# Two tiles per instruction, and copies for every quadrant move, in a batched matmul with bias and residual

## The chip, the cores and the metric

The kernel runs on one core of one Trainium2 chip. Times are device microseconds of one execution. A core has five engines with instruction queues of their own: TensorE (PE, with its weight load PEld), VectorE (DVE), ScalarE (ACT), GpSimd (POOL) and SyncE (SP), which here only issues DMA transfers.

## The reference

```python
batch, m, k, n = 16, 512, 1024, 768        # all float32
out = np.matmul(x, weight) + bias + residual
```

x is 16 x 512 x 1024, so 8192 rows of 1024; weight is 1024 x 768; residual and out are 8192 rows of 768. x is 33.6 MB, residual and out 25.2 MB each, the weight 3.1 MB.

## The kernel before

**Tiles, batches, groups.** The 8192 rows are 64 tiles of 128 rows. Four tiles are a batch (B = 4), eight a group (G = 8). Partition p of a group holds eight consecutive rows of DRAM, and tile j of the group is row j of every partition. x, residual and output are transferred by groups: 4.19 MB for x, 3.15 MB for the others, all issued from SyncE's queue, which issues in program order and waits in front of an issue until its buffer is ready.

**From x to the stationary operand.** TensorE needs x with the contraction on the partitions. Each batch is cast to bf16 by ScalarE (`cast_x`, L110, one cast for each quarter of the contraction, 128x1024 elements), in an order that puts neighbouring contraction elements in pairs, so that two bf16 can be moved as one 32-bit word. VectorE then transposes blocks of 32x32 words, and the blocks are moved between quadrants of 32 partitions. There are sixteen moves (q, m), of 32 partitions x 512 words each. For quarters 0 and 1 VectorE transposes all 128 partitions at once into `tq` (`transpose_blocks`, L124), and ScalarE makes the eight moves as copies (`move_blocks`, L132). For quarters 2 and 3 VectorE transposes each block straight into its place (`transpose_and_move`, L140, eight instructions a batch). The result `xt` has two buffers, `xb` and `tq` one each.

**Matmul and evacuation.** For each tile `matmul` (L149) accumulates eight steps of the contraction in PSUM, each in two chunks, 512 and 256 columns wide. There are four PSUM buffers of a tile each. `evacuate` adds the residual on VectorE (L168) in place in the residual's buffer, and GpSimd then adds the bias (L174, `add_bias`). In group 0 the residual isn't loaded yet: VectorE adds the bias into `o_tile` (L165), and GpSimd adds the residual later (`add_residual`, L178). The bias of the last two tiles is added ahead of time.

**Buffers.** x has two group buffers; the last residual (`r_last`) uses one of them. Four homes of a group each hold the rest: `HOME = [0, 1, 3, 0, 1, 2, 3]` gives the home of residual groups 0 to 6; home 2 starts as `o_tile`, home 3 as the weight's staging buffer. So the load of residual group 3 waits until the last `add_residual` has read group 0 out of home 0, and the load of group 4 until group 1 has been stored.

**Order.** The order on each engine is the program's, written out by hand. In batch b: the matmuls of tile 4b, the whole transposes for batch b+1, the evacuation of the tile before, ScalarE's moves for b+1 and two casts for b+2; then the matmuls of the other three tiles, between which VectorE transposes quarters 2 and 3 into place and evacuates one tile each time. `add_residual` comes at the end of batches 2 and 3, four tiles each, in GpSimd's queue between the bias adds. Transfers follow a table:

```python
moves = {
    1: [(load_x, 3)],
    3: [(load_x, 4), (load_r, 3)],
    4: [(store, 1)],
    5: [(load_x, 5), (load_r, 4), (store, 0)],
    7: [(load_x, 6), (load_r, 5), (store, 2)],
    9: [(load_x, 7), (load_r, 6)],
    11: [(load_r, 7), (store, 3), (store, 4)],
    12: [(store, 5)],
    14: [(store, 6)],
}
```

The functions that the change touches, and what calls them:

Of the kernel before, what the change touches and what calls it, by code (L numbers as in the profile page):

```python
# [7 lines left out]
FP32 = mybir.dt.float32  # L8
BF16 = mybir.dt.bfloat16
U32 = mybir.dt.uint32  # L10
P = 128
Q = 32
G = 8
B = 4
X_BUFS = 2
HOME = [0, 1, 3, 0, 1, 2, 3]
PO_BUFS = 4


@with_exitstack  # L20
def kernel(
# [8 lines left out]
    nc = tc.nc  # L30
# [3 lines left out]
    M, K = x2d.shape  # L34
    N = weight.shape[1]
    R = K // P
    KQ = K // 4
    n_sub = M // P
    n_grp = n_sub // G
    n_bat = n_sub // B  # L40
    chunks = [(0, 512), (512, N - 512)]

    def group(ap, g):

        return ap[g * G * P:(g + 1) * G * P, :].rearrange("(p j) k -> p j k", p=P)

    const = ctx.enter_context(tc.tile_pool(name="const", bufs=1))
    xin_pool = ctx.enter_context(tc.tile_pool(name="xin", bufs=1))
    ring_pool = ctx.enter_context(tc.tile_pool(name="ring", bufs=1))
    xb_pool = ctx.enter_context(tc.tile_pool(name="xbp", bufs=1))  # L50
    xt_pool = ctx.enter_context(tc.tile_pool(name="xtp", bufs=1))
    po_pool = ctx.enter_context(
        tc.tile_pool(name="pop", bufs=1, space=bass.MemoryType.PSUM))

    def o(ins):
        return tc.keep_in_program_order(ins)

    count = {}

    def slot(pool, base, n, shape, dtype, name=None):  # L60
        i = count.get(base, 0)
        count[base] = i + 1
        return pool.tile(shape, dtype, name=name or base, tag=f"{base}{i % n}", bufs=1)

    def home(i, name):
        return ring_pool.tile([P, G, N], FP32, name=name, tag=f"ring{i}", bufs=1)


    bias_rows = const.tile([P, N], FP32, name="bias_rows")
    o(nc.gpsimd.memset(bias_rows, 0.0))  # L70
    warm = const.tile([1, 2], FP32, name="warm")
    o(nc.vector.memset(warm, 0.0))
# [2 lines left out]
    bias_bc = const.tile([P, N], FP32, name="bias_bc")  # L75


    x_tiles, r_tiles, o_tiles = {}, {}, {}

    def load_x(g, j0=0, j1=G):  # L80
        if g not in x_tiles:
            x_tiles[g] = slot(xin_pool, "x_tile", X_BUFS, [P, G, K], FP32)
        o(nc.sync.dma_start(out=x_tiles[g][:, j0:j1, :], in_=group(x2d, g)[:, j0:j1, :]))
# [10 lines left out]
    def store(g, j0=0, j1=G):  # L94
        src = o_tiles[g] if g == 0 else r_tiles[g]
        o(nc.sync.dma_start(out=group(out2d, g)[:, j0:j1, :], in_=src[:, j0:j1, :]))
# [3 lines left out]

    xb_tiles, tq_tiles, xt_tiles, po_tiles = {}, {}, {}, {}

    def cast_x(b, q):

        if b >= n_bat:
            return
        g, j = divmod(b * B, G)
        xb = slot(xb_pool, f"xb{q}_", 1, [P, B, R // 2, Q, 2], BF16)
        part = x_tiles[g][:, j:j + B, q * KQ:(q + 1) * KQ]
        o(nc.scalar.copy(out=xb, in_=part.rearrange("p t (a j r) -> p t j a r", j=R // 2, r=2)))  # L110
        xb_tiles[b, q] = xb.rearrange("p t j a r -> p (t j a r)").bitcast(U32).rearrange(
            "p (t j a) -> p t j a", t=B, j=R // 2)

    def xt_tile(b):
        if b not in xt_tiles:
            xt_tiles[b] = slot(xt_pool, "xt", 2, [P, B, R // 2, P], U32)
        return xt_tiles[b]

    def transpose_blocks(b, q):

        if b >= n_bat:
            return
        tq_tiles[b, q] = slot(xt_pool, f"tq{q}_", 1, [P, B, R // 2, Q], U32)
        o(nc.vector.transpose(out=tq_tiles[b, q], in_=xb_tiles.pop((b, q))))  # L124

    def move_blocks(b, q):

        if b >= n_bat:
            return
        xt, tq = xt_tile(b), tq_tiles.pop((b, q))  # L130
        for m in range(P // Q):
            o(nc.scalar.copy(out=xt[q * Q:(q + 1) * Q, :, :, m * Q:(m + 1) * Q],  # L132
                             in_=tq[m * Q:(m + 1) * Q]))

    def transpose_and_move(b, q):
        if b >= n_bat:
            return
        xt, xb = xt_tile(b), xb_tiles.pop((b, q))
        for m in range(P // Q):
            o(nc.vector.transpose(out=xt[q * Q:(q + 1) * Q, :, :, m * Q:(m + 1) * Q],  # L140
                                  in_=xb[m * Q:(m + 1) * Q]))

    def matmul(t):
        b, i = divmod(t, B)
        xt = xt_tiles[b].bitcast(BF16)[:, i].rearrange("p j (m r) -> p j r m", r=2)
        po_tiles[t] = slot(po_pool, "po", PO_BUFS, [P, N], FP32)
        for k in range(R):
            for (n0, nl) in chunks:
                o(nc.tensor.matmul(  # L149
                    po_tiles[t][:, n0:n0 + nl],  # L150
                    lhsT=xt[:, k // 2, k % 2, :],
                    rhs=w_sb[:, k, n0:n0 + nl],
                    start=(k == 0),
                    stop=(k == R - 1),
                ))

    def evacuate(t):


        if t < 0:  # L160
            return
        g, j = divmod(t, G)
        po = po_tiles.pop(t)
        if g == 0:
            o(nc.vector.tensor_add(out=o_tiles[0][:, j, :], in0=po, in1=bias_bc))  # L165
        else:
            rt = r_tiles[g][:, j, :]
            o(nc.vector.tensor_add(out=rt, in0=po, in1=rt))  # L168
            if t < n_sub - 2:
                add_bias(t)  # L170

    def add_bias(t):
        rt = r_tiles[t // G][:, t % G, :]
        o(nc.gpsimd.tensor_add(out=rt, in0=rt, in1=bias_bc))  # L174

    def add_residual(t):
        ot = o_tiles[0][:, t, :]
        o(nc.gpsimd.tensor_add(out=ot, in0=ot, in1=r_tiles[0][:, t, :]))  # L178


    for p in range(0, P, Q):
# [6 lines left out]
    load_r(1)  # L188
    o_tiles[0] = home(2, "o_tile")
    o(nc.vector.stream_shuffle(out=bias_bc, in_=bias_rows, mask=[0] * 32))  # L190
    for q in range(4):
        cast_x(0, q)
    for q in (0, 1):
        transpose_blocks(0, q)
    for q in (2, 3):
        transpose_and_move(0, q)
    for q in (0, 1):
        move_blocks(0, q)
    for k in range(R):
        if k % 2:  # L200
            o(nc.scalar.copy(out=w_sb[:, k, :], in_=w_stage[:, k, :]))  # L201
        else:
            o(nc.vector.tensor_copy(out=w_sb[:, k, :], in_=w_stage[:, k, :]))  # L203
    for q in range(4):
        cast_x(1, q)
    load_x(2)
    load_r(0)
    load_r(2)
# [13 lines left out]
    for b in range(n_bat):  # L222
        t = B * b
        matmul(t)
        for q in (0, 1):
            transpose_blocks(b + 1, q)
        evacuate(t - 1)
        for q in (0, 1):
            move_blocks(b + 1, q)
        for q in range(4):  # L230
            if q < 2:
                cast_x(b + 2, q)
        matmul(t + 1)
        transpose_and_move(b + 1, 2)
        evacuate(t)
        cast_x(b + 2, 2)
        matmul(t + 2)
        transpose_and_move(b + 1, 3)
        evacuate(t + 1)
        cast_x(b + 2, 3)  # L240
        matmul(t + 3)
        evacuate(t + 2)
        if b in (2, 3):
            for u in range(B * (b - 2), B * (b - 1)):
                add_residual(u)
        if b == n_bat - 3:
            for u in (n_sub - 2, n_sub - 1):
                add_bias(u)
        if b == n_bat - 1:
            store(n_grp - 1, 0, B)  # L250
        for move, *what in moves.get(b, []):
            move(*what)
    evacuate(n_sub - 1)
    store(n_grp - 1, B, B + 2)
    store(n_grp - 1, B + 2, G)
# [1 line left out]
_INS = ['x', 'weight', 'bias', 'residual']  # L257
# [26 lines left out]
```

## Time and profile before

| | |
|---|---|
| median of 3 runs | 211.26 us (210.24 to 211.74) |
| the profiled execution's own time | 210.11 us |
| its span, first to last instruction | 208.3 us |
| mean granted TensorE clock | 0.974 |
| busy: TensorE, VectorE, ScalarE, GpSimd | 171.5, 171.0, 151.4, 115.3 us |
| main transfer queue | 87.03 MB, 97.9% of 16 engines' span |
| HBM | 61.88 MB read, 25.17 MB written |

How to read the rows. A row of digits cuts the span into 40 slices of 5.2 us; a digit is the busy share in tenths, 9 being 90% or more. A group's line names the source line, engine, operation and operands, then "busy us, mean ns of one | idle time of the engine just before them, and what ended it". A line of a timeline has start, duration, engine, source line, operation, operands and how many instructions were merged; an idle time before it stands in brackets with its releaser. The waits of the queue are in us: total, times, longest. `SPq` lines are the issues of transfers, not the transfers themselves.

### The profile page before, as it was taken

The page shows a single profiled execution, that of the slowest core. Times are in us where ns is not written, and L with a number is a line of the kernel's source. Part 1 is how long each engine was busy: PE and PEld are TensorE (multiplying, and loading weights), DVE is VectorE, ACT ScalarE, POOL GpSimd, SP SyncE. Part 2 cuts the span into 40 slices and gives each one's busy share as a digit, 9 for nine tenths or more (in the row PEclk, how much of TensorE's full clock was granted, in tenths as well). Part 3 has the DMA queues.
Part 4 walks back from the last instruction along what each step waited for, and adds up shares of the span by engine and source line. Part 5 has one row for each costly group of instructions (what it writes and reads, how often), then busy time and mean ns, then how long its engine had stood idle before and what let it go on. Part 6 is the DMA issues. An engine that isn't in the chain of part 4 may idle for free.

```text
span 208.3 us, 2737 instructions
## 1 busy us (share of the span) xinstructions
PE 171.5 (82%) x1004; PEld 101.2 (49%) x1024; DVE 171.0 (82%) x231; ACT 151.4 (73%) x198; POOL 115.3 (55%) x69
## 2 busy tenths in 40 slices
PE   0002999999999999999999599996999589999940
PEld 0001566666666656565656256663656246666620
DVE  0089799999999999999995999949997699997320
ACT  2499999999797599897979579783979569750000
POOL 1000000003899999999764493916766376699900
PEclk9999999999999999999999979999999969999996
DMA  6999999999999999999999999999999999999995
GB/s 245 452 409 437 466 415 403 475 400 431 423 458 409 415 469 373 411 434 437 437 406 444 440 437 417 417 445 442 425 423 415 448 426 437 415 448 415 430 405 211
DMA packets 4053, 87.22 MB, mean 419 GB/s; under 512 B 452, under 2 KB 452, under 8 KB 712
## 3 DMA queue, kind: packets, MB, share of 16 engines
q1 hardware_dynamic: 4032, 87.03, 97.9%
q8 instruction: 8, 0.13, 0.2%
q14 instruction: 5, 0.04, 0.0%
q10 hardware_dynamic: 8, 0.01, 0.0%
HBM read 61.88 MB, written 25.17 MB: 418 GB/s over the span
## 4 chain that ended last, share of the span: by engine, by line
DMA 44%; DVE 26%; PE 16%; POOL 5%; issue 3%; ACT 2%; SPq 0%; ACTq 0%; DVEq 0%
DMA out_dram<-r_tile 20%; PE po L149 16%; DVE xt L140 14%; DMA out_dram<-o_tile 12%; DMA r_tile<-in_residual_dram 8%; DMA bias_rows<-in_bias_dram 4%; DVE r_tile L168 4%; POOL o_tile L178 3%; DVE o_tile L165 3%; POOL r_tile L174 2%; DVE w_sb L203 1%; ACT L73 1%; ACT xb__132 L110 1%; ACT xb__136 L110 0%; DVE bias_bc L190 0%
## 5 line engine op out<-in xcount | busy, mean ns | idle before, releaser
L149 PE MATMUL po<-w_sb,xt 128*128 128x512 bf16 (+1 forms) x1004 | 171.5, 331 | 28.5 <-DVE w_sb L203 19.8
L149 PEld LDWEIGHTS <-xt 128*128 128x128 bf16 x1024 | 101.2, 99 | 98.5 <-ACT w_sb L201 19.2
L174 POOL TENSOR_TENSOR r_tile<-r_tile,bias_bc 128x768 f32<-128x768 f32 x48 | 86.0, 1814 | 82.6 <-DVE r_tile L168 82.6
L168 DVE TENSOR_TENSOR r_tile<-po,r_tile 128x768 f32<-128x768 f32 x48 | 44.4, 946 | 9.1 <-DMA r_tile<-in_residual_dram 8.4
L178 POOL TENSOR_TENSOR o_tile<-o_tile,r_tile 128x768 f32<-128x768 f32 x8 | 14.3, 1825 | 0.0
L174 POOL TENSOR_TENSOR r_last<-r_last,bias_bc 128x768 f32<-128x768 f32 x8 | 14.3, 1810 | 0.0
L168 DVE TENSOR_TENSOR r_last<-po,r_last 128x768 f32<-128x768 f32 x8 | 7.5, 955 | 6.2 <-PE po L149 6.1
L190 DVE LOAD_MASK_SELECT bias_bc<-bias_rows x1 | 0.0, 14 | 10.3 <-DMA bias_rows<-in_bias_dram 10.3
L165 DVE TENSOR_TENSOR o_tile<-po,bias_bc 128x768 f32<-128x768 f32 x8 | 7.4, 945 | 0.1
L110 ACT CAST xb__95<-x_tile 128x1024 bf16<-128x1024 f32 x1 | 1.1, 1107 | 6.0 <-DMA x_tile<-in_x_dram 6.0
L132 ACT COPY xt<-tq__1018 32x512 uint32<-32x512 uint32 x4 | 2.5, 618 | 1.4 <-DVE tq__1018 L124 1.3
L132 ACT COPY xt<-tq__1232 32x512 uint32<-32x512 uint32 x4 | 2.5, 617 | 1.4 <-DVE tq__1232 L124 1.3
L132 ACT COPY xt<-tq__1552 32x512 uint32<-32x512 uint32 x4 | 2.5, 617 | 1.4 <-DVE tq__1552 L124 1.3
L132 ACT COPY xt<-tq__1659 32x512 uint32<-32x512 uint32 x4 | 2.5, 617 | 1.4 <-DVE tq__1659 L124 1.3
L132 ACT COPY xt<-tq__1337 32x512 uint32<-32x512 uint32 x4 | 2.5, 617 | 1.4 <-DVE tq__1337 L124 1.3
L132 ACT COPY xt<-tq__1446 32x512 uint32<-32x512 uint32 x4 | 2.5, 617 | 1.4 <-DVE tq__1446 L124 1.3
L132 ACT COPY xt<-tq__474 32x512 uint32<-32x512 uint32 x4 | 2.5, 616 | 1.4 <-DVE tq__474 L124 1.3
L132 ACT COPY xt<-tq__1123 32x512 uint32<-32x512 uint32 x4 | 2.5, 616 | 1.4 <-DVE tq__1123 L124 1.3
L132 ACT COPY xt<-tq__587 32x512 uint32<-32x512 uint32 x4 | 2.5, 618 | 1.4 <-DVE tq__587 L124 1.3
L132 ACT COPY xt<-tq__908 32x512 uint32<-32x512 uint32 x4 | 2.5, 616 | 1.4 <-DVE tq__908 L124 1.3
L110 ACT CAST xb__1299<-x_tile 128x1024 bf16<-128x1024 f32 x1 | 1.1, 1137 | 3.0 <-DVE xt L140 3.0
L110 ACT CAST xb__1513<-x_tile 128x1024 bf16<-128x1024 f32 x1 | 1.1, 1131 | 2.9 <-DVE xt L140 2.9
(158 smaller groups left out, 244.0 us busy)
## 6 DMA issues: line engine op xcount, KB each, us to landing
x_tile<-in_x_dram SPq DMA_DIRECT2D x7, 4096.0 KB, 23.2
r_tile<-in_residual_dram SPq DMA_DIRECT2D x7, 3072.0 KB, 17.0
out_dram<-r_tile SPq DMA_DIRECT2D x6, 3072.0 KB, 20.7
x_tile<-in_x_dram SPq DMA_DIRECT2D x2, 2048.0 KB, 13.1
w_stage<-in_weight_dram SPq DMA_DIRECT2D x1, 3072.0 KB, 14.4
out_dram<-o_tile SPq DMA_DIRECT2D x1, 3072.0 KB
r_last<-in_residual_dram SPq DMA_DIRECT2D x1, 3072.0 KB, 15.7
out_dram<-r_last SPq DMA_DIRECT2D x1, 1536.0 KB, 8.9
```

Source lines behind the costliest of these rows:

```text
L73: o(nc.scalar.copy(out=warm, in_=warm))
L110: o(nc.scalar.copy(out=xb, in_=part.rearrange("p t (a j r) -> p t j a r", j=R // 2, r=2)))
L132: o(nc.scalar.copy(out=xt[q * Q:(q + 1) * Q, :, :, m * Q:(m + 1) * Q], in_=tq[m * Q:(m + 1) * Q]))
L140: o(nc.vector.transpose(out=xt[q * Q:(q + 1) * Q, :, :, m * Q:(m + 1) * Q], in_=xb[m * Q:(m + 1) * Q]))
L149: o(nc.tensor.matmul(po_tiles[t][:, n0:n0 + nl], lhsT=xt[:, k // 2, k % 2, :], rhs=w_sb[:, k, n0:n0 + nl], start=(k == 0), stop=(k == R - ...
L165: o(nc.vector.tensor_add(out=o_tiles[0][:, j, :], in0=po, in1=bias_bc))
L168: o(nc.vector.tensor_add(out=rt, in0=po, in1=rt))
L174: o(nc.gpsimd.tensor_add(out=rt, in0=rt, in1=bias_bc))
L178: o(nc.gpsimd.tensor_add(out=ot, in0=ot, in1=r_tiles[0][:, t, :]))
L203: o(nc.vector.tensor_copy(out=w_sb[:, k, :], in_=w_stage[:, k, :]))
```

## The change

ScalarE casts two tiles in one instruction, the whole contraction at once (two casts of 128x2048 elements for a batch in place of four of 128x1024). VectorE transposes all 128 partitions of both halves (two instructions of 128x1024 words), and there is no transpose into place any more: all sixteen moves are copies, of which VectorE makes the first nine and ScalarE the last seven. `tq` holds a whole batch. A PSUM buffer holds two tiles, and there are two of them; evacuations and GpSimd's adds take two tiles in one instruction, the last two tiles apart. In a batch VectorE evacuates the pair before, transposes, copies, and then evacuates the batch's first pair. All adds of residual group 0 are issued on GpSimd in batch 2, ahead of the bias adds of tiles 8 and on. The bias rows' staging takes home 0 in place of a buffer of its own. The table of transfers is the same.

```diff
-PO_BUFS = 4
+H = 2
...
-    KQ = K // 4
+    J = R // 2
...
-    bias_rows = const.tile([P, N], FP32, name="bias_rows")
+    bias_rows = home(0, "bias_rows")[:, 0, :]
...
-    def cast_x(b, q):
+    def cast_x(b, h):
         if b >= n_bat:
             return
...
+        g, i = divmod(b * B + h * H, G)
+        xb = slot(xb_pool, f"xb{h}_", 1, [P, H, J, P, 2], BF16)
+        o(nc.scalar.copy(out=xb, in_=x_tiles[g][:, i:i + H, :].rearrange(
+            "p t (c j r) -> p t j c r", j=J, r=2)))
+        xb_tiles[b, h] = xb.rearrange("p t j c r -> p (t j c r)").bitcast(U32)
+
+    def transpose_blocks(b, h):
...
+        if h == 0:
+            tq_tiles[b] = slot(xt_pool, "tq", 1, [P, B * J * P], U32)
+        n = H * J * P
+        o(nc.vector.transpose(out=tq_tiles[b][:, h * n:(h + 1) * n], in_=xb_tiles.pop((b, h))))
+
+    def move_blocks(b, engine, n):
...
+            xt_tiles[b] = slot(xt_pool, "xt", 2, [P, B * J, P], U32)
+        tq = tq_tiles[b].rearrange("p (tj q a) -> p tj q a", q=P // Q, a=Q)
+        for _ in range(n):
+            i = count.get(("move", b), 0)
+            count["move", b] = i + 1
+            q, m = divmod(i, P // Q)
+            out_ = xt_tiles[b][q * Q:(q + 1) * Q, :, m * Q:(m + 1) * Q]
+            in_ = tq[m * Q:(m + 1) * Q, :, q, :]
+            if engine is nc.scalar:
+                o(engine.copy(out=out_, in_=in_))
+            else:
+                o(engine.tensor_copy(out=out_, in_=in_))
...
-        po_tiles[t] = slot(po_pool, "po", PO_BUFS, [P, N], FP32)
+        if t % H == 0:
+            po_tiles[t // H] = slot(po_pool, "po", 2, [P, H, 1024], FP32)
+        po = po_tiles[t // H][:, t % H, :]
...
+    def bias_for(n):
+        return bias_bc[:, None, :].broadcast_to([P, n, N])
+
+    def evacuate(t, n=H):
...
+        po = po_tiles[t // H][:, t % H:t % H + n, :N]
         if g == 0:
+            o(nc.vector.tensor_add(out=o_tiles[0][:, i:i + n, :], in0=po, in1=bias_for(n)))
         else:
+            rt = r_tiles[g][:, i:i + n, :]
             o(nc.vector.tensor_add(out=rt, in0=po, in1=rt))
             if t < n_sub - 2:
+                add_bias(t, n)
...
+    def add_bias(t, n=H):
+        i = t % G
+        rt = r_tiles[t // G][:, i:i + n, :]
+        o(nc.gpsimd.tensor_add(out=rt, in0=rt, in1=bias_for(n)))
+
+    def add_residual(t, n=H):
+        ot = o_tiles[0][:, t:t + n, :]
+        o(nc.gpsimd.tensor_add(out=ot, in0=ot, in1=r_tiles[0][:, t:t + n, :]))
...
+    for h in (0, 1):
+        cast_x(0, h)
+        transpose_blocks(0, h)
+    move_blocks(0, nc.vector, 9)
+    move_blocks(0, nc.scalar, 7)
...
+    for h in (0, 1):
+        cast_x(1, h)
...
         matmul(t)
...
         matmul(t + 1)
+        evacuate(t - H)
+        if t == G:
+            for u in range(0, G, H):
+                add_residual(u)
+        transpose_blocks(b + 1, 0)
+        transpose_blocks(b + 1, 1)
+        move_blocks(b + 1, nc.vector, 9)
+        move_blocks(b + 1, nc.scalar, 7)
+        cast_x(b + 2, 0)
+        matmul(t + 2)
+        matmul(t + 3)
         evacuate(t)
+        cast_x(b + 2, 1)
         if b == n_bat - 3:
+            add_bias(n_sub - 2)
...
-    evacuate(n_sub - 1)
+    evacuate(n_sub - 2, 1)
     store(n_grp - 1, B, B + 2)
+    evacuate(n_sub - 1, 1)
     store(n_grp - 1, B + 2, G)
```

More of the change, by code (lines that the diff above doesn't have):

```diff
@@ L101 @@
     xb_tiles, tq_tiles, xt_tiles, po_tiles = {}, {}, {}, {}
-    def cast_x(b, q):
+    def cast_x(b, h):
         if b >= n_bat:
             return
[L107 to L119, printed above, removed]
+        g, i = divmod(b * B + h * H, G)
[3 more added lines that the diff above has]
+        xb_tiles[b, h] = xb.rearrange("p t j c r -> p (t j c r)").bitcast(U32)
@@ L121, in transpose_blocks @@
+    def transpose_blocks(b, h):
         if b >= n_bat:
             return
-        tq_tiles[b, q] = slot(xt_pool, f"tq{q}_", 1, [P, B, R // 2, Q], U32)
-        o(nc.vector.transpose(out=tq_tiles[b, q], in_=xb_tiles.pop((b, q))))
-    def move_blocks(b, q):
+        if h == 0:
[3 more added lines that the diff above has]
+    def move_blocks(b, engine, n):
@@ L128, in move_blocks @@
         if b >= n_bat:
             return
[L130 to L141, printed above, removed]
+        if b not in xt_tiles:
+            xt_tiles[b] = slot(xt_pool, "xt", 2, [P, B * J, P], U32)
@@ L143, in matmul @@
     def matmul(t):
         b, i = divmod(t, B)
-        xt = xt_tiles[b].bitcast(BF16)[:, i].rearrange("p j (m r) -> p j r m", r=2)
-        po_tiles[t] = slot(po_pool, "po", PO_BUFS, [P, N], FP32)
+        xt = xt_tiles[b][:, i * J:(i + 1) * J, :].bitcast(BF16).rearrange(
+            "p j (m r) -> p j r m", r=2)
+        if t % H == 0:
+            po_tiles[t // H] = slot(po_pool, "po", 2, [P, H, 1024], FP32)
+        po = po_tiles[t // H][:, t % H, :]
         for k in range(R):
@@ L149, in matmul @@
                 o(nc.tensor.matmul(
-                    po_tiles[t][:, n0:n0 + nl],
+                    po[:, n0:n0 + nl],
                     lhsT=xt[:, k // 2, k % 2, :],
@@ L155, in matmul @@
                 ))
-    def evacuate(t):
+    def bias_for(n):
+        return bias_bc[:, None, :].broadcast_to([P, n, N])
+    def evacuate(t, n=H):
         if t < 0:
             return
-        g, j = divmod(t, G)
-        po = po_tiles.pop(t)
+        g, i = divmod(t, G)
+        po = po_tiles[t // H][:, t % H:t % H + n, :N]
         if g == 0:
-            o(nc.vector.tensor_add(out=o_tiles[0][:, j, :], in0=po, in1=bias_bc))
+            o(nc.vector.tensor_add(out=o_tiles[0][:, i:i + n, :], in0=po, in1=bias_for(n)))
         else:
-            rt = r_tiles[g][:, j, :]
+            rt = r_tiles[g][:, i:i + n, :]
             o(nc.vector.tensor_add(out=rt, in0=po, in1=rt))
             if t < n_sub - 2:
[L170 to L178, printed above, removed]
+                add_bias(t, n)
[6 more added lines that the diff above has]
+        o(nc.gpsimd.tensor_add(out=ot, in0=ot, in1=r_tiles[0][:, t:t + n, :]))
     for p in range(0, P, Q):
@@ L190 @@
     o(nc.vector.stream_shuffle(out=bias_bc, in_=bias_rows, mask=[0] * 32))
[L191 to L198, printed above, removed]
+    for h in (0, 1):
[3 more added lines that the diff above has]
+    move_blocks(0, nc.scalar, 7)
     for k in range(R):
@@ L203 @@
             o(nc.vector.tensor_copy(out=w_sb[:, k, :], in_=w_stage[:, k, :]))
-    for q in range(4):
-        cast_x(1, q)
+    for h in (0, 1):
+        cast_x(1, h)
     load_x(2)
@@ L224 @@
         matmul(t)
[L225 to L232, printed above, removed]
-        matmul(t + 1)
-        transpose_and_move(b + 1, 2)
-        evacuate(t)
[L236 to L245, printed above, removed]
+        matmul(t + 1)
+        evacuate(t - H)
[9 more added lines that the diff above has]
+        matmul(t + 3)
+        evacuate(t)
+        cast_x(b + 2, 1)
         if b == n_bat - 3:
-            for u in (n_sub - 2, n_sub - 1):
-                add_bias(u)
+            add_bias(n_sub - 2)
         if b == n_bat - 1:
```

## The prediction

> **What bounds the kernel now.** I read the page's head first (the span, the busy shares, the transfer row, the queue), then the queue's own waits, then the timelines of SyncE, GpSimd and VectorE, and last the groups by shape.
>
> ```profile
> span 208.3 us, 2737 instructions
> PE 171.5 (82%) x1004; PEld 101.2 (49%) x1024; DVE 171.0 (82%) x231; ACT 151.4 (73%) x198; POOL 115.3 (55%) x69
> DMA  6999999999999999999999999999999999999995
> q1 hardware_dynamic: 4032, 87.03, 97.9%
> ```
>
> No engine is above 82%, but the transfers are at 97.9% with no gap in the row. 87.03 MB, from about 2.1 us to about 205.5 us, is 0.428 MB/us. So the span is the stream, 203.4 us, with about 2 us ahead of it and 3 us behind. An engine's saving brings nothing; an engine can only hurt, by issuing a transfer after the stream has run dry. So the question is which issue comes late, and how much lies queued in front of it.
>
> ```profile
> SPq L96 <- POOL r_tile L174: 29.8, 3, 24.6
> SPq L92 <- POOL o_tile L178: 13.7, 1, 13.7
> ```
>
> ```profile
> 78.03 0.33 SPq L92 DMA_DIRECT2D r_tile<-in_residual_dram  x1
> 79.81 0.35 SPq L96 DMA_DIRECT2D out_dram<-r_tile  x1
> 86.11 0.33 SPq L83 DMA_DIRECT2D x_tile<-in_x_dram  x1
> ```
>
> SyncE issues in program order. The load of residual group 3 (78.03) stands behind the last of eight L178 adds, since it reuses the first residual's buffer; the store of group 1 (79.81) stands behind the bias add of tile 15. What was issued through that load is 5 x groups, the weights and 4 residual groups, 20.97 + 3.15 + 12.58 = 36.70 MB, which lasts until 2.1 + 36.70/0.428 = 87.8 us. So this store has some 8 us to spare, less 1.4 us from issue to first byte. This is the tightest place at which GpSimd decides.
>
> ```profile
> 49.20 1.83 POOL L174 TENSOR_TENSOR r_tile<-r_tile,bias_bc 128x768 f32<-128x768 f32 x1 [47.73 <-DVE r_tile L168]
> 53.08 3.59 POOL L174 TENSOR_TENSOR r_tile<-r_tile,bias_bc 128x768 f32<-128x768 f32 x2 [2.05 <-DVE r_tile L168]
> 56.62 7.17 POOL L178 TENSOR_TENSOR o_tile<-o_tile,r_tile 128x768 f32<-128x768 f32 x4
> ```
>
> GpSimd is idle until 49.20 and then adds without a pause; four adds start 7.14 us apart (56.62, 63.74), so 1.785 us a tile.
>
> ```profile
> L203 DVE CAST w_sb<-w_stage 128x768 bf16<-128x768 f32 x4 | 2.0, 556 | 0.0
> L140 DVE STREAM_TRANSPOSE xt<-xb__432 32x512 uint32<-32x512 uint32 x4 | 2.8, 706 | 0.1
> L168 DVE TENSOR_TENSOR r_tile<-po,r_tile 128x768 f32<-128x768 f32 x48 | 44.4, 946 | 9.1 <-DMA r_tile<-in_residual_dram 8.4
> L165 DVE TENSOR_TENSOR o_tile<-po,bias_bc 128x768 f32<-128x768 f32 x8 | 7.4, 945 | 0.1
> ```
>
> The mean of one is the number behind the busy time. VectorE's adds cost the same beside a working GpSimd (946 ns) as beside an idle one (945); L140 costs 705 in both. The L203 cast is another kind: 768 elements in 556 ns where a transpose takes 705 for 512, so it passes about twice as many elements in its time as the others. All four L203 casts ran before 21.1 us, beside an idle GpSimd. No row shows this fast kind beside a GpSimd add.
>
> **The change part by part, for a batch of four tiles.**
>
> ```profile
> 53.78 0.70 DVE L124 STREAM_TRANSPOSE tq__474<-xb__380 128x512 uint32<-128x512 uint32 x1
> 54.40 0.67 DVE L124 STREAM_TRANSPOSE tq__476<-xb__382 128x512 uint32<-128x512 uint32 x1
> ...
> 64.45 0.70 DVE L124 STREAM_TRANSPOSE tq__587<-xb__489 128x512 uint32<-128x512 uint32 x1
> ```
>
> VectorE before: two whole transposes 0.61 us apart, eight L140 at 0.715 us, four adds at 0.94: 1.2 + 5.7 + 3.8 = 10.7, and the first transposes of two batches start 10.67 us apart (53.78, 64.45). After: two transposes of 1024 elements, between 0.71 and 1.24 us each (one row, or two spaced rows); I take 1.2. Two adds of two tiles, at most 2 x 0.945; I take 1.75, one fixed part saved. Nine copies 32x512: at least 0.556 x 512/768 = 0.37, at most L140's 0.715; nearest is L203's fast kind (one input, one output, both on chip), so 0.43, between 0.37 and 0.556. Sum 2.4 + 3.5 + 3.9 = 9.8 us, or 12.3 us with copies at 0.715.
>
> ScalarE: the casts started 1.03 us apart for 1024 elements; one of 2048 takes at most 2.06, I take 1.9. The moves are spaced 0.627 (four in 2.51). Before 4 x 1.03 + 8 x 0.627 = 9.1; after 3.8 + 4.4 = 8.2. It stays under the rest.
>
> TensorE: the last four evacuations, which wait for it alone, start 2.62 us apart, so 10.5 us a batch. The stream needs 5.24 MB a batch (2.10 x, 1.57 residual, 1.57 store), 12.2 us. With 9.8 on VectorE and 10.5 on TensorE the compute stays below 12.2, and all savings lie under the stream. PSUM in two pairs means that a pair must be evacuated before the batch after can start; at 9.8 us that is done in time.
>
> Start: matmuls of a batch now need both transposes and all sixteen moves; I put the first batches 1 to 2 us later. The load of x group 2 has 11 us of queue in front of it (14.68 MB issued by 24.97, some 9.8 moved), so nothing is lost.
>
> GpSimd's order: all eight residual adds stand ahead of the bias adds of tiles 8 to 15. They wait for residual group 0: x, weights, x, residual 1, x, residual 0 is 22.02 MB, 2.1 + 51.4 + 1.5 to land = 55.0 (group 6 by the same sum lands at 162.9, and its VectorE add starts at 163.23). GpSimd starts at 55.0 in place of 49.2. The load of group 3 now waits for 14.3 us of adds, to 69.4, and is issued 8.6 us earlier than at 78.03. The store of group 1 comes after 16 x 1.785 = 28.6 us, at 83.7 and 3.9 us later than now, still ahead of 87.8 - 1.4 = 86.4. Its margin is 2.7 us. Behind it in SyncE's queue stand x group 5, residual 4 (which waits for this store to land) and the store of group 0.
>
> Copies beside adds: the cost that no row shows. From below: nothing, each runs as if alone (a gain has no source, since neither gets shorter). From above: a copy and an add exclude each other. The nearest rows lie on neither end: the slow kinds on VectorE are free of GpSimd, the fast kind was never beside it. I take exclusion, because the fast kind moves twice the data of every row that was seen to be free, and each add is one instruction of 3.57 us that a copy can fall into.
>
> The Trainium skill (SBUF — State Buffer, section Who interferes with whom) states that VectorE's two-port modes, copies among them, and GpSimd hold one port pair by turns, each for a whole instruction while the other stands still; no run here shows it. By that rule the sum is the forecast below, and without it that of the first rival.
>
> With exclusion, from 55.0 on GpSimd and the copies share one resource. If the nine copies run together when their turn comes, a batch takes 7.14 of adds + 3.9 of copies = 11.1 us there. Four batches' copies fall into the stretch: 28.6 + 4 x 3.9 = 44.3, so the store of group 1 is issued at 99.3. The stream has run dry at 87.8 and starts again at 100.7: 13 us lost. Later GpSimd catches up, and a batch is a chain on VectorE: evacuation 1.75, its add 3.57, the next evacuation's add 3.57 (transposes and evacuation lie under these), copies 3.9: 12.8 us. After the last residual wait about two of them run 1.8 us over TensorE's pace, 3.5 us more. Sum 13.0 + 3.5 = 16.5: span 224.8. The profiled execution took 210.11 for its 208.3, so 226.6, and the median shown (211.26) is 1.15 above it: about 227.5. I say 227.
>
> **The rivals.**
>
> No collision (not slower): copies and adds run side by side. For it: all other pairs in this trace do. Against it: above. The store goes at 83.7, before 86.4, every later issue has 3 us or more in front of it, the stream never runs dry: 208.3 again, 210 to 212. It decides as long as 28.6 us of adds are stretched by less than 2.7 us.
>
> Strict turns: exclusion, but after each copy the waiting add goes first. At the batch that starts at 54.4, six adds are queued; the copies wait through all: 55.0 + 6 x 3.57 + 3.9 + evacuation 1.75 = 82.2 for the next batch, 17 us late. From there 12.85 us a batch, 82.2 + 11 x 12.85 = 223.5, some 3.6 for adds queued at the end, the last batch 10.5 and its store 7: 244.6 on the stream's clock where now it is 206.7. That is 38 more, 249. For it: adds start back to back, 30 ns before the one before has ended (1.785 against 1.815), which leaves a copy no gap. Against it: nothing but that it needs this order of turns.
>
> Slow copies: 0.715 each without collision. VectorE needs 12.3 us a batch, above 12.2: the last batch starts at 209, plus 10.5 and a store of 7: 226.5 against 206.7, 230. For it: the copies have the shape of L140, 32 partitions. Against it: L203.
>
> Faster: there are about 2 us of unused transfer time in the head and 3 in the tail, and nothing in the change touches the first load or the last store's bytes. At most 1 to 2 us.
>
> **How the numbers follow.** Forecast 0.38, no collision 0.37, strict turns 0.14, slow copies 0.07, faster 0.04. The two first are near each other, since only the missing row tells them apart. The forecast's own range is 218 to 236 (copies 0.37 to 0.556, one or two batches more or less in the stretch). The range from 209 to 243 takes in the first rival and leaves out most of strict turns and of faster. One per cent, 2.1 us, is about what a measurement of this kernel can tell from no change (its runs span 1.5 us). Slower by more than that: 0.38 + 0.14 + 0.07 and 0.03 of the first rival's upper edge, 0.62; within it 0.34; faster 0.04.
>
> **What would show it.** Right: VectorE copies near 0.43 us in batches 0 and 1, and stretched to several times that, or GpSimd's adds stretched beyond 3.6 us, after 55; the store of group 1 near 99; the transfer row below 9 in the slices from 88 to 100. Residual group 3 issued before 78 shows the new order at work in every case. Wrong: copies of 0.43 beside adds of 3.57 throughout, the store before 87 and a full row (first rival); copies of 0.7 from the start (slow copies); TensorE idle for 15 us or more near 65 to 82 (strict turns).

## The result, and the profile after

The changed kernel takes 241.92 us (median of 6 runs, 240.97 to 242.13) against 210.37 of the kernel before in the same series: a ratio of 1.1475, 95% interval 1.1433 to 1.1517. It is slower by 31.5 us. The profiled execution has a span of 238.8 us, 30.5 more than before.

The head of the page after:

```profile
span 238.8 us, 2601 instructions
...
DMA  7999999999999999039999999999927999948366
...
q1 hardware_dynamic: 4032, 87.03, 87.2%
```

The same 87.03 MB now have holes: the stream runs dry in slices 17 and 18 (from about 95 us), again in the thirties, and at the end. The table by stretches of 6 us sizes two of the holes (its columns: stretch, length, busy time of TensorE, its weight load, VectorE, ScalarE and GpSimd, granted clock, the transfers' share, GB/s):

```profile
96.00:102.00 6.00, 5.95 (x38) 3.59 (x37) 5.90 (x7) 4.87 (x8) 3.86 (x2) 1.00 0.00 0
102.00:108.00 6.00, 4.07 (x26) 2.36 (x25) 5.93 (x7) 3.46 (x2) 2.55 (x1) 1.00 0.33 87
...
174.00:180.00 6.00, 4.11 (x25) 2.44 (x25) 5.86 (x11) 5.94 (x6) 0.47 (x1) 1.00 0.12 49
```

That is 10.0 us without transfers in the first two rows (6.0, and 0.67 of 6) and 5.3 in the third; VectorE is full in all of them. Most of the rest of the 30.5 us lies near the end, where the last batches come late: the transfers' share is 0.30 from 210 to 216 us and 0.17 from 222 to 228. The costliest groups say with what VectorE is busy (mean ns of one behind the busy time):

```profile
L137 DVE COPY xt<-tq 32x512 uint32<-32x512 uint32 x144 | 111.0, 771 | 2.2
L177 POOL TENSOR_TENSOR r_tile<-r_tile,bias_bc 128x1536 f32<-128x1536 f32 x24 | 82.7, 3467 | 59.4 <-DVE r_tile L170 53.7
...
L170 DVE TENSOR_TENSOR r_tile<-po,r_tile 128x1536 f32<-128x1536 f32 x24 | 41.3, 1753 | 1.1 <-PE po L148 0.7
```

A copy takes 771 ns in the mean; the median is 417 and the longest takes 3585. VectorE's timeline of batch 3, in short windows, so that the copies are not merged, and GpSimd's of the same time:

```profile
57.80 1.71 DVE L137 COPY xt<-tq 32x512 uint32<-32x512 uint32 x1
59.53 3.57 DVE L137 COPY xt<-tq 32x512 uint32<-32x512 uint32 x1
63.11 3.58 DVE L137 COPY xt<-tq 32x512 uint32<-32x512 uint32 x1
...
73.83 3.54 DVE L137 COPY xt<-tq 32x512 uint32<-32x512 uint32 x1
77.38 0.42 DVE L137 COPY xt<-tq 32x512 uint32<-32x512 uint32 x1
```

```profile
59.19 3.64 POOL L181 TENSOR_TENSOR o_tile<-o_tile,r_tile 128x1536 f32<-128x1536 f32 x1
62.77 3.65 POOL L181 TENSOR_TENSOR o_tile<-o_tile,r_tile 128x1536 f32<-128x1536 f32 x1
...
96.43 3.43 POOL L177 TENSOR_TENSOR r_tile<-r_tile,bias_bc 128x1536 f32<-128x1536 f32 x1
```

Each copy that starts beside an add ends about 0.3 us after the next add has started (59.53 + 3.57 = 63.10, against 62.77), and the next copy waits for that add in turn. Six copies go this way through the queue of six adds; when it is empty, at 77.1 (the sixth copy ends at 77.37), the last three take 0.42 each. Nine copies take 20.9 us in this batch.

From then on a batch takes about 12.44 us: VectorE's first copies of later batches start at 84.43, 96.99, 109.35, 121.79 and 134.23, and each first one takes some 3.2 us, since it waits for the second of the two adds just released. That fits the chain 1.75 (an evacuation) + 2 x 3.42 (two adds) + 3.85 (nine copies) = 12.44. The queue of transfers shows what became late:

```profile
70.00 0.33 SPq L92 DMA_DIRECT2D r_tile<-in_residual_dram  x1
87.40 0.35 SPq L96 DMA_DIRECT2D out_dram<-r_tile  x1
105.49 0.33 SPq L83 DMA_DIRECT2D x_tile<-in_x_dram  x1
```

Residual group 3 goes out 8 us earlier than before, the store of group 1 at 87.40, and x group 5 at 105.49 in place of 86.11, since it waits for the casts of a batch that is late (17.7 us of that wait in SyncE's queue). In front of it the stream dried up.

### The profile page after: what moved, and what is told of

Same layout as the page of the kernel before. It is cut to its first block, busy times and chain, and to the rows that moved or that the text cites. A ratio compares the mean times of both kernels' runs of the same rounds, so it can differ in the third digit from the quotient of the medians.

```text
span 238.8 us, 2601 instructions
## 1 busy us (share of the span) xinstructions
PE 173.1 (72%) x1004; PEld 101.8 (43%) x1024; DVE 206.0 (86%) x216; ACT 137.8 (58%) x150; POOL 111.4 (47%) x37
## 3 DMA queue, kind: packets, MB, share of 16 engines
q1 hardware_dynamic: 4032, 87.03, 87.2%
## 4 chain that ended last, share of the span: by engine, by line
DVE 60%; PE 14%; issue 10%; ACT 5%; DMA 3%; POOL 3%; POOLq 1%; DVEq 0%; ACTq 0%
DVE xt L137 38%; PE po L148 14%; DVE tq L119 12%; DVE r_tile L170 7%; DMA bias_rows<-in_bias_dram 3%; POOL r_last L177 3%; ACT xt L135 2%; POOLq L272 1%; DVE r_last L170 1%; ACT w_sb L201 1%; ACT xb__129 L108 1%; ACT xb__127 L108 1%; DVE o_tile L167 1%; ACT L73 1%; DVE bias_bc L193 0%
## 5 line engine op out<-in xcount | busy, mean ns | idle before, releaser
L137 DVE COPY xt<-tq 32x512 uint32<-32x512 uint32 x144 | 111.0, 771 | 2.2
L177 POOL TENSOR_TENSOR r_tile<-r_tile,bias_bc 128x1536 f32<-128x1536 f32 x24 | 82.7, 3467 | 59.4 <-DVE r_tile L170 53.7
L135 ACT COPY xt<-tq 32x512 uint32<-32x512 uint32 x112 | 68.9, 615 | 68.5 <-DVE tq L119 67.3
L170 DVE TENSOR_TENSOR r_tile<-po,r_tile 128x1536 f32<-128x1536 f32 x24 | 41.3, 1753 | 1.1 <-PE po L148 0.7
L181 POOL TENSOR_TENSOR o_tile<-o_tile,r_tile 128x1536 f32<-128x1536 f32 x4 | 14.2, 3584 | 54.3 <-DMA r_tile<-in_residual_dram 54.3
L177 POOL TENSOR_TENSOR r_last<-r_last,bias_bc 128x1536 f32<-128x1536 f32 x4 | 13.7, 3434 | 7.2 <-DVE r_last L170 7.2
L170 DVE TENSOR_TENSOR r_last<-po,r_last 128x1536 f32<-128x1536 f32 (+1 forms) x5 | 7.0, 1433 | 9.0 <-PE po L148 5.5
L167 DVE TENSOR_TENSOR o_tile<-po,bias_bc 128x1536 f32<-128x1536 f32 x4 | 6.9, 1754 | 1.0 <-PE po L148 0.9
L108 ACT CAST xb__95<-x_tile 128x2048 bf16<-128x2048 f32 x1 | 2.0, 2026 | 5.9 <-DMA x_tile<-in_x_dram 5.9
L201 ACT CAST w_sb<-w_stage 128x768 bf16<-128x768 f32 x4 | 3.0, 828 | 0.0
L108 ACT CAST xb__572<-x_tile 128x2048 bf16<-128x2048 f32 x1 | 2.1, 2086 | 0.0
L108 ACT CAST xb__1438<-x_tile 128x2048 bf16<-128x2048 f32 x1 | 2.1, 2078 | 0.0
L108 ACT CAST xb__860<-x_tile 128x2048 bf16<-128x2048 f32 x1 | 2.1, 2077 | 0.0
L108 ACT CAST xb__1151<-x_tile 128x2048 bf16<-128x2048 f32 x1 | 2.1, 2077 | 0.0
L108 ACT CAST xb__959<-x_tile 128x2048 bf16<-128x2048 f32 x1 | 2.1, 2077 | 0.0
L108 ACT CAST xb__1053<-x_tile 128x2048 bf16<-128x2048 f32 x1 | 2.1, 2077 | 0.0
L108 ACT CAST xb__1343<-x_tile 128x2048 bf16<-128x2048 f32 x1 | 2.1, 2077 | 0.0
L108 ACT CAST xb__474<-x_tile 128x2048 bf16<-128x2048 f32 x1 | 2.1, 2075 | 0.0
## 6 DMA issues: line engine op xcount, KB each, us to landing
out_dram<-r_tile SPq DMA_DIRECT2D x6, 3072.0 KB, 17.7
```

The source lines that it names most:

```text
L108: o(nc.scalar.copy(out=xb, in_=x_tiles[g][:, i:i + H, :].rearrange("p t (c j r) -> p t j c r", j=J, r=2)))
L135: o(engine.copy(out=out_, in_=in_))
L137: o(engine.tensor_copy(out=out_, in_=in_))
L167: o(nc.vector.tensor_add(out=o_tiles[0][:, i:i + n, :], in0=po, in1=bias_for(n)))
L177: o(nc.gpsimd.tensor_add(out=rt, in0=rt, in1=bias_for(n)))
L181: o(nc.gpsimd.tensor_add(out=ot, in0=ot, in1=r_tiles[0][:, t:t + n, :]))
```

## The experiments

The theory, from the trace above (**turns**), is that a VectorE copy and a GpSimd add exclude each other, one instruction at a time. Its rivals are **merging** (two-tile instructions and pairs hand over later), **order** (the residual's adds come first), and copies that are slow by themselves. Of each edit the lines that matter are shown; `...` stands for what is left out.

**The copies undone, all else kept.**

```diff
-                o(engine.tensor_copy(out=out_, in_=in_))
+                o(nc.vector.transpose(out=out_, in_=words(b)[m * Q:(m + 1) * Q, :, q, :]))
```

This line is for quarters 2 and 3 (`words(b)` is the cast batch as 32-bit words, in one buffer). Quarters 0 and 1 are transposed whole, one instruction each, and all eight of their moves are ScalarE's, one more than in the changed kernel.

> The changed kernel with only its VectorE copies undone: two-tile casts, two-tile adds on both engines, PSUM pairs and the first residual's adds first all stay; the eight moves of quarters 2 and 3 are transposes into place again (0.71 us each), the other eight are ScalarE copies. Turns (a VectorE copy and a GpSimd add exclude each other, one instruction at a time): no fast VectorE instruction is left after the weight casts, so the whole loss goes, 209 to 213 us, VectorE's transposes stay at 0.71 and GpSimd's adds at 3.57 beside each other. Merging (the loss comes from two-tile instructions and pairs, which hand over later): the loss stays for its larger part, 230 us or more. Order (the loss comes from the residual's adds ahead of the bias adds): it stays too, above 225.

Measured 212.85 us, ratio 1.0101 (1.0069 to 1.0133). The loss of 31.5 falls to about 2.6. Its transposes into place, in a kernel whose adds take 3465 ns:

```profile
L137 DVE STREAM_TRANSPOSE xt<-xb 32x512 uint32<-32x512 uint32 x128 | 90.2, 704 | 2.0
```

Merging and order, which are both still in this kernel, are out as main causes. The 1% left was not taken apart; in this version the casts wait 9.4 us in all for the transposes of the single buffer that the edit needed.

**The adds left out, the copies kept.**

```diff
-        o(nc.gpsimd.tensor_add(out=rt, in0=rt, in1=bias_for(n)))
+        return
...
-        o(nc.gpsimd.tensor_add(out=ot, in0=ot, in1=r_tiles[0][:, t:t + n, :]))
+        return
```

> The changed kernel without GpSimd's adds (the bias of groups 1 to 7 and the residual of group 0 are left out); everything else stays, the nine copies too. Turns: every copy takes 0.42 to 0.43 us, no wait of 1 us or more in the copies, the stream is full again: 208 to 211 us. Slow or strided copies, or merging: the copies or hand-overs cost the same as before, 235 to 242.

Measured 209.90 us, ratio 0.9971 (0.9954 to 0.9988). The 144 copies:

```profile
L137 DVE COPY xt<-tq 32x512 uint32<-32x512 uint32 x144 | 60.0, 417 | 2.2
```

The copies alone are as cheap as the prediction took them, and with nothing beside them the kernel is back at the stream's time. It also shows how little there was to win: even with all of GpSimd's adds gone, the changed kernel is only 0.3% faster than the kernel before. What another order of the transfers could bring was not tried.

**A slower instruction for the same move.**

```diff
-                o(engine.tensor_copy(out=out_, in_=in_))
+                o(engine.stream_shuffle(out=out_, in_=in_, mask=list(range(Q))))
```

> The changed kernel with each of the nine VectorE copies made by a stream_shuffle with the identity mask, same operands: a slower instruction, 0.71 us at one element a step in place of 0.42. Turns, tied to the fast kind: the shuffles run beside the adds without a wait, VectorE's sum is 2.3 + 3.5 + 9 x 0.72 = 12.3 us a batch, a little over the stream's 12.2; 226 to 231 us, so faster than the changed kernel although each instruction is 0.3 us longer. If any VectorE move between quadrants excludes the adds, whatever its rate: waits as before and longer instructions, 255 to 280.

Measured 228.09 us, ratio 1.0832 (1.0807 to 1.0857). All 144 lie between 698 and 745 ns (the line gives min/median/max):

```profile
L137 DVE STREAM_SHUFFLE xt<-tq x144: 698/719/745, 14.6 to 206.9; 32x512 uint32<-32x512 uint32 x144
```

An instruction 70% longer makes the kernel 13.8 us faster than the copy, since it never waits. Its operands and its place in the order are those of the copy, so no dependency between instructions makes the copies wait. What is left of the loss goes with VectorE's own sum: VectorE is busy for 198.1 of 226.1 us, and the evacuations start 12.4 us apart (58.62, 71.05, 83.49), just over the stream's 12.2. How the 17.9 us divide between this pace and the two ends of the run was not taken apart.

**The copies alone, in the kernel before.**

```diff
     def transpose_and_move(b, q):
...
+        transpose_blocks(b, q)
...
-            o(nc.vector.transpose(out=xt[q * Q:(q + 1) * Q, :, :, m * Q:(m + 1) * Q],
-                                  in_=xb[m * Q:(m + 1) * Q]))
+            o(nc.vector.tensor_copy(out=xt[q * Q:(q + 1) * Q, :, :, m * Q:(m + 1) * Q],
+                                    in_=tq[m * Q:(m + 1) * Q]))
```

> The kernel before with one part of the change alone: quarters 2 and 3 are transposed whole into tq on VectorE (0.61) and moved by four VectorE copies each, in place of four transposes into place each. One-tile adds, four PSUM buffers, the old order of the residual's adds, the old casts; bias_rows lies in home 0 to make room. On paper VectorE's batch falls from 10.7 to 2.4 + 8 x 0.43 + 3.8 = 9.7 us. Turns: each copy waits for up to one add of 1.79; two batches late by some 8 us each near 52 to 88, then 12.5 us a batch; 228 to 236 us. Merging or order: neither is in here, so 209 to 212.

Measured 231.06 us, ratio 1.0971 (1.0930 to 1.1012). Four copies that would take 1.7 us without a wait take 4.9 and 6.3:

```profile
55.07 4.90 DVE L141 COPY xt<-tq__526 32x512 uint32<-32x512 uint32 x4
...
61.61 6.26 DVE L141 COPY xt<-tq__553 32x512 uint32<-32x512 uint32 x4
```

This one part of the change, alone, brings 20.8 of the 31.5 us.

**Rate, or second read?**

```diff
-                o(engine.tensor_copy(out=out_, in_=in_))
+                o(engine.tensor_tensor(out=out_, in0=in_, in1=in_, op=mybir.AluOpType.bitwise_or))
```

> The changed kernel with each VectorE copy made by a two-input instruction at one element a step, the bitwise or of the block with itself (both inputs on chip memory). It asks what makes a VectorE instruction exclude the adds: its rate, or its second read. Rate only: 0.72 us beside the adds as the shuffles had, 226 to 231 us. Second read: it waits its turn like the copies, and is longer itself; the steady batch is 3.57 + 3.57 + 9 x 0.72 + 1.75 = 15.3 us, 272 to 282 us. The Trainium skill (SBUF — State Buffer, section Who interferes with whom) states the second, for two inputs in SBUF against a GpSimd instruction that reads SBUF.

Measured 271.63 us, ratio 1.2896 (1.2870 to 1.2921).

```profile
L137 DVE TENSOR_TENSOR xt<-tq x144: 678/681/3861, 14.4 to 248.3; 32x512 uint32<-32x512 uint32 x144
```

The time is just under the second expectation's 272. At 681 ns the instruction is about as slow as the shuffle, yet it waits, up to 3861. So a slow rate doesn't keep an instruction out of the collision. Two kinds waited beside adds here: the fast copy, and the slow instruction with two inputs in on-chip memory. Three did not: the shuffle, the transpose, and the add whose other input is in PSUM. The Trainium skill (SBUF — State Buffer, section Who interferes with whom) names both kinds, two-port copies and two-input instructions, as excluding GpSimd; the runs agree with it on which kinds wait (3585 and 3861 ns at most). That it is a second port by which the fast copy collides, no run here shows.

**GpSimd that only writes.**

```diff
-        o(nc.gpsimd.tensor_add(out=rt, in0=rt, in1=bias_for(n)))
+        for _ in range(2):
+            o(nc.gpsimd.memset(rt, 0.0))
```

and the same for the residual's adds.

> The changed kernel with each two-tile add on GpSimd replaced by two memsets of the same region (the first residual and the bias are left out, and what the adds would have read is overwritten): GpSimd writes and reads nothing; some 1.4 us each from the 0.74 us of the 768-element memset at the start. Whole exclusion: copies wait for memsets as they waited for adds, some copies of 1 us and more, 218 to 226 us. Exclusion by the read side alone: copies of 0.42 throughout and a full stream, 209 to 212.

Measured 210.09 us in one run, against 210.66 for the kernel before. The time fits the second expectation, the trace the first:

```profile
L137 DVE COPY xt<-tq x144: 414/418/1583, 14.5 to 187.7; 32x512 uint32<-32x512 uint32 x144
```

Copies wait for memsets too, up to about one memset (1424 ns in the mean; the longest copy took 1583), so it is not only GpSimd's reads that keep them out. The estimate of 218 to 226 was wrong because it kept the queue of the adds: a memset doesn't wait for the first residual to land, so none was piled up at 56 us, and a batch (nine copies in 5.1 us, 10.9 us in all) stays under 12.2. So waits of this size cost nothing here as long as the batch fits under the stream.

**One-tile adds**, and **the old order of the residual's adds**.

```diff
-        o(nc.gpsimd.tensor_add(out=rt, in0=rt, in1=bias_for(n)))
+        for u in range(n):
+            o(nc.gpsimd.tensor_add(out=rt[:, u, :], in0=rt[:, u, :], in1=bias_bc))
```

> The changed kernel with each two-tile add on GpSimd split into two of one tile; the copies and all else stay. Turns: each copy waits for a shorter add, but there are twice as many to wait for and the same 1.75 us a tile stand between transposes and moves; near 56 us all nine copies wait for 1.8 each in place of six for 3.6, 16 in place of 21 us; 236 to 241 us. Merging (the length of one add is what hurts): half of the loss goes, below 228.

```diff
-        if t == G:
-            for u in range(0, G, H):
-                add_residual(u)
...
+        if b in (2, 3):
+            for u in range(B * (b - 2), B * (b - 1), H):
+                add_residual(u)
```

> The changed kernel with the residual's adds back where they were: two after the bias adds of batch 2, two after those of batch 3. Turns: the adds that the copies meet are the same in number, only spread over two batches, while residual group 3 is issued later again (near 80 in place of 70); 238 to 243 us, no clear gain. Order (putting them first made the queue of six adds that the copies ran into): the stall near 60 to 77 goes and the time falls to 230 or less.

The one-tile adds took 239.11 us (ratio 1.1359, 1.1332 to 1.1385), the old order 239.35 (1.1366, 1.1341 to 1.1391). Nine copies of batch 3 take 17.3 us with one-tile adds. With the old order the stall is spread over two batches:

```profile
57.90 12.26 DVE L137 COPY xt<-tq 32x512 uint32<-32x512 uint32 x9
75.92 13.00 DVE L137 COPY xt<-tq 32x512 uint32<-32x512 uint32 x9
```

Each is worth about 3 us of 31.5, so neither the length of an add nor its place in the queue makes the loss. What the variants have in common is the GpSimd work that the copies stand behind: six adds of two tiles (20.9 us for nine copies), nine of one tile (17.3), or the same adds spread over two batches (12.3 and 13.0).

**Six copies in place of nine.**

```diff
-        move_blocks(b + 1, nc.vector, 9)
-        move_blocks(b + 1, nc.scalar, 7)
+        move_blocks(b + 1, nc.vector, 6)
+        move_blocks(b + 1, nc.scalar, 10)
```

> The changed kernel with six moves on VectorE and ten on ScalarE in place of nine and seven. Turns: a batch's chain is an evacuation 1.75, two adds of 3.42, six copies of 0.43, 11.2 us, now under the stream's 12.2, so after the stall near 60 to 80, where all six copies still wait for the queue of adds, nothing is lost in the later batches; 224 to 230 us. Cost by the copy (each copy loses the same, wherever it meets an add): 31.5 us of loss x 6/9 = 21, 231 to 233 us, and the batches stay near 12.4 us less a third of what they lost.

Measured 229.64 us, ratio 1.0918 (1.0886 to 1.0950), inside the first expectation, but it doesn't tell cleanly. The stall is there (six copies in 13.77 us), and later copies wait less, in the end not at all (3.0 and 2.6 us for six at 119.57 and 131.35, where 2.6 is the time without a wait). But ScalarE's chain now sets the batch:

```profile
107.89 6.26 ACT L135 COPY xt<-tq 32x512 uint32<-32x512 uint32 x10 [1.37 <-PE po L148]
```

Ten moves in 6.26 us, two casts in 4.1 and a wait of 1.4 for TensorE to leave the buffer are 11.75 us. The split of nine and seven was not compared at equal load on ScalarE.

## Why the prediction was right or wrong

**The bound: right.** The stream sets the time as long as it is full, and all savings lie under it: with the collisions gone the kernel takes 209.9.

**The prices: nearly all right.** Copies 0.43 apart (0.417 long); evacuations 1.753 (taken 1.75); transposes 1.15 to 1.25 apart (1.2). Casts were 2.08 in place of 1.9, without effect. Two-tile adds took 3.42 alone, where 2 x 1.785 = 3.57 was taken.

**The order of the residual's adds: right.** GpSimd started at 55.79 (55.0), residual group 3 went out at 70.00 (69.4).

**Copies beside adds: the right end was taken.** Exclusion was chosen at 0.38 against no collision at 0.37, from little more than that the pair had never been seen together. The two runs that take away one side each (209.90 without adds, 212.85 without copies) and the shuffles show it. The reason that the prediction added, that the fast kind moves twice the data of the slow ones, turned out not to be needed: the bitwise or is about as slow as the shuffle (681 against 719 ns) and waits all the same.

**The step that failed is the order of turns**, "if the nine copies run together when their turn comes". They don't: a copy starts only when the one before has ended, and by then the next add has begun. So the case that happened is the rival "strict turns", which had a chance of 0.14, and the sign that was named for it, TensorE idle for 15 us or more near 65 to 82, is in the trace:

```profile
80.51 14.76 PE L148 MATMUL po<-w_sb,xt 128*128 128x512 bf16 x76 [16.41 <-DVE r_tile L170]
```

The forecast let four batches' copies through in 44 us. In the run the first batch alone kept its copies for 20.9 us, and the batches behind it, at 12.44 us against the stream's 12.2, could make up nothing. So the two terms of the sum came out otherwise. The dry stretch put at 13.0 us, in front of the store of group 1 (99.3), measured 10.0 and lies in front of x group 5, with the store already out at 87.40. Some 20 of the 30.5 us were lost after it, where the forecast had 3.5.

The rival's own working mostly holds: the batch after the stall was to start at 82.2, and TensorE took up again at 80.51; a batch was to take 12.85 and took 12.44. Its 249 was 7 too high: 4.5 us of it are the shorter time of eleven batches (3.3 of that the adds, two of 0.15 less in each), 1.7 the earlier end of the stall; the rest, about 1 us, was not taken apart.

So 227 was short by 15 us. That 241.9 still lies within the range given, near its upper end, is luck: the forecast's own range ended at 236, and the whole range was meant to leave out most of strict turns, whose price was too high.

The trace of before had a hint that was used for the rival alone: adds followed each other without a gap. What it could not show is how copies follow each other. The four fast casts of L203 overlap there (four of 556 ns in 1.97 us), while the copies do not (0.43 us apart, 0.42 long); why the two differ, no run here shows.

Two slips in the prediction carry little weight. GpSimd does pause once more after 49.20, for 2.05 us before 53.08, as the line shown there says. And 12.8 against TensorE's 10.5 is 2.3 us a batch, not 1.8, so that the 3.5 us should have been 4.6.

## What to carry to other kernels

A copy on VectorE with both ends in on-chip memory is priced by what GpSimd does at the same time: here it cost up to a whole GpSimd instruction (3.58 us in place of 0.42). Where GpSimd adds run beside it, a slower instruction that does not wait for them (a transpose into place, a shuffle) can be the better one: 228 us with shuffles against 242 here, and 213 with the transposes. And before an engine is made faster, see whether it bounds anything: here the stream did, and even without GpSimd's adds the change won 0.3%.

## What the runs showed of the hardware

Turns are taken by instruction, and they are not even: a waiting copy of 0.42 us stands for the whole add of 3.4, while an add behind a copy starts only 0.16 to 0.21 us later (3.56 to 3.61 between starts in the stall, 3.40 without). The Trainium skill (SBUF — State Buffer, section Who interferes with whom) has the loser stand still for the whole instruction of the other; for the copies the trace agrees, for the adds it shows less than the copy's 0.42, and the measurement decides. Which part of its 0.42 us a copy keeps the add out, no run here shows.

After TensorE had stood idle from about 64 to 80.5 us its granted clock was 0.50 in the stretches from 72 to 84 and 0.98 in that from 84 to 90. It had hardly a part in the loss, since VectorE's chain was nearly untouched by it: the two evacuations from 91.13 on took 3.55 us in place of 3.42.
